# Eight floats of padding ahead of the large on-chip tile of a hybrid decoder kernel

## The chip, the cores and the metric

The kernel runs on one core of a Trainium2 chip. Its time is the device time of one execution in microseconds (us); the median of three runs before the change is 3118.18 us (3116.29 to 3118.25). One further execution was profiled; the trace and all durations below are from it.

## The reference

The computation is a decoder trunk in float32: 256 tokens of width 1024 pass four layers, and each layer is a token mixer followed by an expert network. The mixers are, in order, HGRN2 (a gated linear recurrence in chunks), FoX (attention with a forget gate), Mamba-2 SSD, and HGRN2 again.

```
for i in range(DEPTH):                                   # 4 layers
    hn = rmsnorm(h, norm_mix[i])
    h = h + mixer_i(hn)                                  # HGRN2, FoX, SSD, HGRN2
    h = h + peer_ffn(rmsnorm(h, norm_ffn[i]), ...)
return rmsnorm(h, norm_final)

def peer_ffn(h, w_q, sub_keys, u_tab, v_tab):            # in blocks of 128 tokens
    q = (xb @ w_q).reshape(M, 8, 2, 128)                 # 8 heads, two half queries
    s = einsum('mhcd,hckd->mhck', q, sub_keys)           # 128 keys per half
    ...                                                  # top 16 of the 16 x 16 sums: idx, gates
    u = take(u_tab, idx); v = take(v_tab, idx)           # 16 experts per token and head
    act = gelu(einsum('md,mhkd->mhk', xb, u)) * gates
    return einsum('mhk,mhkd->md', act, v)
```

The expert network is what moves the bytes: for each of 256 tokens, 8 heads, 16 experts and 4 layers one row of u (1024 floats) and one of v is read from a table in HBM, 8 KB together, and each row is used once.

## The kernel before

**Storage.** Nearly everything that lives in the on-chip memory lies in one tile of 196,864 bytes per partition, called `arena` (line 208), cut by hand into pieces (lines 206 to 212): the residual stream `h`, two transposed or repeated copies of the tokens (`xT`, `XR`), the keys, the scores `SS`, a work area `mix` for the mixers, `kept` (eight places of 8 KB that hold weights across the two token blocks of a layer) and `gb` (seven buffers of 8 KB). The tile is the fourth of its pool, behind the constants `cst` (3,136 bytes per partition), the parameters `par` (1,544) and the identity with the norm weights `fst` (768). Two streaming buffers `raw` of 8 KB per partition lie in a pool behind it, and the small working tiles in another behind that. Each piece of `arena` has a length that is a multiple of 256 bytes, so all pieces begin at the same place within a block of 256 bytes as the tile itself. In the program as built, `arena` begins at byte 7,648 of each partition, which is 29 blocks of 256 bytes and 224 bytes more; the `raw` buffers begin at bytes 205,024 and 213,216, also 224 bytes past a multiple of 256. Places are given out in steps of 32 bytes.

**Gathers.** A pair is 2 × 64 tokens with two experts each. For each half of a pair (`g`), `fetch` (line 1519) takes a free buffer of 8 KB per partition from a deque `ring`, and GpSimd issues one indirect DMA (line 1517) that brings 128 rows of 8 KB, u and v side by side, one row into each partition: 1 MB. The buffers of the ring are the seven of `gb`, and those of the eight kept places that no weight holds at the time. The last pair of all is fetched in six smaller gathers (`fetch_last`).

**What is done with a buffer.** `dot` (line 1550): VectorE multiplies the u half with the token's row and sums it (the call at line 1554, recorded at the helper's line 229). `active`: ScalarE applies the gelu and scales a 128 × 64 matrix with it (line 242). `spread` (line 1574): TensorE multiplies that matrix with the v half into the accumulators (line 1587), after which the buffer goes back to the ring (line 1590). The loop over pairs (line 1713) has 64 pairs in each of 8 stages; a stage is one block of 128 tokens of one layer.

**Beside it.** While one stage gathers, the mixer and the queries of the next run in pieces between the pairs (`side`, `products_`, `others`), by a table of costs. Their weights come in units of 1 MB through SyncE's queue (line 413), into the two `raw` buffers, the kept places, or, in the beginning, other pieces of the arena. The routing of the next heads (top 16, indices, gates) runs in steps on VectorE (`route_steps`). The order of all instructions on each engine is fixed when the program is built.

Of the kernel before, what the change touches and what calls it, by code (L numbers as in the profile page):

```python
# [11 lines left out]
F32 = mybir.dt.float32  # L12
# [7 lines left out]
P = 128  # L20
# [169 lines left out]
def trunk(ctx: ExitStack, tc: tile.TileContext, d: dict, out: bass.AP):  # L190
    nc = tc.nc
    SB = bass.MemoryType.PSUM
    cpool = ctx.enter_context(tc.tile_pool(name="c", bufs=1))
# [11 lines left out]
    fst = cpool.tile([P, P + 8 * 2 * DEPTH], F32, name="fst")  # L205
    sizes = (("h", D), ("xT", D), ("XR", 2 * D), ("keys", UNIT), ("SS", 2048), ("mix", MIX), ("kept", NKEPT * UNIT),
             ("gb", NGB * 2 * D))
    arena = cpool.tile([P, sum(n for _, n in sizes)], F32, name="arena")
    at_, o_ = {}, 0
    for name, n in sizes:  # L210
# [1556 lines left out]
```

## Time and profile before

| what | number |
|---|---|
| median of three runs | 3118.18 us |
| the profiled execution | 3123.27 us, its span from the first to the last instruction 3121.4 us |
| instructions | 34,341 |
| mean granted TensorE clock | 0.942 |
| busy: TensorE, VectorE, ScalarE, GpSimd | 83%, 67%, 50%, 39% of the span |
| moved by DMA | 1266.60 MB, mean 406 GB/s |
| gathers | 1028 indirect DMAs, 1073.81 MB |
| loads and stores through SyncE's queue | 190.60 MB |

The page of the profile gives busy times of the engines, the span in 40 equal slices (a digit is a share in tenths, GB/s is what the DMA moved in that slice), the DMA queues with their packets, the chain of work that ended last, and the groups of instructions. A packet is one piece of a transfer that one of the core's 16 DMA engines carries out: here a row of a partition, or the four bytes that report a DMA's end. Since every DMA over 128 partitions is spread over 16 engines, each of them gets 8 rows and one such report. The share of a queue is the sum of its packets' times over 16 engines times the stretch; records of neighbouring packets overlap a little, so it can pass 100%.

### The profile page before, as it was taken

How to read it: one execution, taken by the hardware profiler on the slowest of the kernel's cores; microseconds unless marked ns; L12 is line 12 of the kernel's file. 1: busy time of each engine (PE TensorE's matmuls, PEld its weight loads, DVE VectorE, ACT ScalarE, POOL GpSimd, SP SyncE). 2: the span in 40 equal slices, each digit the busy share in tenths (PEclk: the TensorE clock that was granted, in tenths of full speed). 3: DMA queues.
4: the chain of work that ended last, by engine and by line, in shares of the span. 5: the costliest groups of instructions: out<-in, count | busy, mean ns of one | idle time of the engine just before them, and what ended most of it. 6: DMA issues, size and time to landing. Idle time of an engine off the chain costs nothing.

```text
span 3121.4 us, 34341 instructions
## 1 busy us (share of the span) xinstructions
PE 2592.7 (83%) x10170; PEld 1106.6 (35%) x10170; DVE 2103.5 (67%) x5583; ACT 1563.6 (50%) x4485; POOL 1202.7 (39%) x1036
## 2 busy tenths in 40 slices
PE   9899877987789996898878998869887899876666
PEld 4444342332234552344324543523222343521111
DVE  1677657765857766888486885577657677677754
ACT  3465434463445643688245784346444655443433
POOL 0244334443433342433243333334334333455454
PEclk9999988999899998999989999989989999999999
DMA  8799999999999999999999999999999999999998
GB/s 339 280 418 420 419 419 414 414 407 420 411 412 419 386 416 419 391 418 420 388 419 411 407 419 383 412 413 401 419 420 419 410 408 419 419 419 420 420 420 345
DMA packets 176184, 1266.60 MB, mean 406 GB/s; under 512 B 19584, under 2 KB 20224, under 8 KB 22912
## 3 DMA queue, kind: packets, MB, share of 16 engines
q0 software_dynamic: 147776, 1073.81, 83.8%
q1 hardware_dynamic: 28224, 190.60, 14.9%
q8 instruction: 84, 1.38, 0.2%
q14 instruction: 100, 0.82, 0.1%
HBM read 1263.28 MB, written 1.05 MB: 405 GB/s over the span
## 4 chain that ended last, share of the span: by engine, by line
DMA 47%; PE 18%; issue 14%; DVE 11%; POOL 5%; ACT 4%; POOLq 0%; DVEq 0%
DMA arena<-in_uv,ix 46%; PE pj L271 8%; DVE arena L229 7%; PE acc L1587 6%; POOL arena L1517 5%; PE ps L271 4%; ACT L242 2%; DMA raw<-in_ssm 1%; DVE eq L229 1%; ACT dg L242 1%; ACT arena L242 1%; PE ps L275 1%; DVE af L229 0%; DMA arena<-in_wq 0%; DVE gs L229 0%
## 5 line engine op out<-in xcount | busy, mean ns | idle before, releaser
L1517 POOL DMA_INDIRECT arena<-in_uv,ix x1028 | 1200.4, 1168 | 1902.3 <-PE acc L1587 1189.2
L229 DVE SCALAR_TENSOR_TENSOR arena<-arena 128x1024 f32<-128x1024 f32 (+2 forms) x1088 | 1267.6, 1172 | 825.4 <-DMA arena<-in_uv,ix 817.0
L1587 PE MATMUL acc<-arena,dg 128*64 128x512 f32 x4096 | 1389.0, 662 | 471.5 <-ACT dg L242 469.3
L242 ACT ACTIVATE dots<-dots 128x1 f32<-128x1 f32 x1024 | 203.0, 198 | 1242.8 <-DVE arena L229 1241.4
L1587 PEld LDWEIGHTS acc<-arena,dg 128*64 128x64 f32 x4096 | 343.2, 144 | 1333.8 <-ACT dg L242 936.1
L271 PE MATMUL pj<-arena 128*128 128x128 f32 (+1 forms) x1760 | 435.7, 400 | 1.5 <-ACT arena L242 0.8
L242 ACT ACT_TABLE_LOAD x330 | 423.4, 1283 | 6.9 <-PEq L1758 0.7
L271 PE MATMUL pj<-raw,arena 128*128 128x512 f32 x736 | 352.3, 620 | 29.6 <-DMA raw<-in_ssm 24.5
L242 ACT ACTIVATE dg<-dg,dots 128x64 f32<-128x64 f32 x1024 | 356.2, 348 | 33.2
L271 PEld LDWEIGHTS pj<-arena 128*128 128x128 f32 x1760 | 246.1, 191 | 184.4 <-issue 169.3
L242 ACT ACTIVATE dg<-m,gs 128x64 f32<-128x64 f32 x1024 | 293.8, 334 | 0.0
L271 PE MATMUL ps<-arena 128*128 128x128 f32 (+4 forms) x1696 | 232.7, 284 | 4.2 <-DMA arena<-in_wq 2.1
L271 PEld LDWEIGHTS ps<-arena 128*128 128x128 f32 (+3 forms) x1696 | 188.6, 177 | 107.5 <-issue 54.6
L271 PEld LDWEIGHTS pj<-raw,arena 128*128 128x128 f32 x736 | 134.6, 194 | 244.9 <-issue 209.2
L242 ACT ACTIVATE arena<-ps 128x256 f32<-128x256 f32 (+4 forms) x186 | 64.8, 391 | 45.3 <-PE ps L271 44.7
L229 DVE DVE_READ_ACCUMULATOR arena<-arena 128x1 f32 x1024 | 83.8, 82 | 0.0
L271 PE MATMUL ps<-cst,arena 128*128 128x128 f32 (+2 forms) x320 | 73.3, 343 | 0.4 <-DVE arena L229 0.4
L275 PEld LDWEIGHTS ps<-fst,arena 128*128 128x128 f32 x440 | 51.5, 146 | 58.4 <-issue 36.4
L275 PE MATMUL ps<-fst,arena 128*128 128x128 f32 x440 | 70.5, 288 | 0.7 <-DVE arena L229 0.7
L229 DVE FIND_INDEX8 si<-sv,arena 128x8 uint32<-128x128 f32 x256 | 69.8, 284 | 0.0
L229 DVE MAX8 sv<-arena 128x8 f32<-128x128 f32 x256 | 61.5, 282 | 4.0 <-ACT arena L242 4.0
L229 DVE SCALAR_TENSOR_TENSOR arena<-arena,cst 128x128 f32<-128x128 f32 x224 | 62.3, 345 | 0.3
(132 smaller groups left out, 1415.3 us busy)
## 6 DMA issues: line engine op xcount, KB each, us to landing
raw<-in_ssm SPq DMA_DIRECT2D x48, 1024.0 KB, 9.3
arena<-in_hg SPq DMA_DIRECT2D x31, 1024.0 KB, 19.7
raw<-in_hg SPq DMA_DIRECT2D x30, 1024.0 KB, 9.3
arena<-in_wq SPq DMA_DIRECT2D x21, 1024.0 KB, 10.0
arena<-in_uv,ix POOLq DMA_INDIRECT x1028, 13.3
raw<-in_fox SPq DMA_DIRECT2D x14, 1024.0 KB, 9.6
raw<-in_wq SPq DMA_DIRECT2D x9, 1024.0 KB, 9.1
arena<-in_fox SPq DMA_DIRECT2D x9, 1024.0 KB, 14.8
```

Of the source, the lines that this page charges most:

```text
L229: return getattr(nc.vector, name)(o, *a, **k)
L242: nc.scalar.activation(o, i, f, **k)
L271: nc.tensor.matmul(o, w, m, start=start, stop=stop)
L275: nc.tensor.transpose(o, i, ident)
L1517: nc.gpsimd.indirect_dma_start(o, None, src, bass.IndirectOffsetOnAxis(ap=ix, axis=0))
L1587: nc.tensor.matmul(accs[s][e][g * 64:g * 64 + 64], dg[:, g], v, start=False, stop=hh == 7 and q == NQ - 1)
```

## The change

One tile of eight floats (32 bytes) per partition, which nothing reads or writes, is put between `fst` and `arena`. In the program as built `arena` then begins at byte 7,680 (30 × 256), the `raw` buffers at 205,056 and 213,248 (801 and 833 × 256); with them every piece of `arena`, the seven ring buffers and the kept places begin at multiples of 256 bytes. The small tiles behind move up by 32 bytes too; `cst`, `par` and `fst` stay. The sequence of instructions on each of the five engines is the same, row for row, with shapes and order unchanged; only line numbers behind line 207 grow by one.

```
     sizes = (("h", D), ("xT", D), ("XR", 2 * D), ("keys", UNIT), ("SS", 2048), ("mix", MIX), ("kept", NKEPT * UNIT),
              ("gb", NGB * 2 * D))
+    cpool.tile([P, 8], F32, name="pad")
     arena = cpool.tile([P, sum(n for _, n in sizes)], F32, name="arena")
     at_, o_ = {}, 0
     for name, n in sizes:
```

More of the change, by code (lines that the diff above doesn't have):

```diff
@@ L207, in trunk @@
              ("gb", NGB * 2 * D))
+    cpool.tile([P, 8], F32, name="pad")
     arena = cpool.tile([P, sum(n for _, n in sizes)], F32, name="arena")
```

## The prediction

> **What bounds the kernel now.** I read first the page's slices, queues and DMA total.
>
> ```profile
> PE 2592.7 (83%) x10170; PEld 1106.6 (35%) x10170; DVE 2103.5 (67%) x5583; ACT 1563.6 (50%) x4485; POOL 1202.7 (39%) x1036
> ...
> GB/s 339 280 418 420 419 419 414 414 407 420 411 412 419 386 416 419 391 418 420 388 419 411 407 419 383 412 413 401 419 420 419 410 408 419 419 419 420 420 420 345
> DMA packets 176184, 1266.60 MB, mean 406 GB/s; under 512 B 19584, under 2 KB 20224, under 8 KB 22912
> ...
> q0 software_dynamic: 147776, 1073.81, 83.8%
> q1 hardware_dynamic: 28224, 190.60, 14.9%
> ```
>
> Most slices stand at 418 to 420 GB/s and none passes that; in between are dips to 383 or 391. At 420 GB/s the 1266.60 MB would take 1266.60 / 0.420 = 3016 us of the span's 3121.4: all but 105 us is at the pace of the transfers. No engine is as full as that. Then the chain of work that ended last:
>
> ```profile
> DMA 47%; PE 18%; issue 14%; DVE 11%; POOL 5%; ACT 4%; POOLq 0%; DVEq 0%
> DMA arena<-in_uv,ix 46%; PE pj L271 8%; DVE arena L229 7%; PE acc L1587 6%; POOL arena L1517 5%; PE ps L271 4%; ACT L242 2%; DMA raw<-in_ssm 1%; DVE eq L229 1%; ACT dg L242 1%; ACT arena L242 1%; PE ps L275 1%; DVE af L229 0%; DMA arena<-in_wq 0%; DVE gs L229 0%
> ```
>
> By this only 47% of the span, 1467 us, is surely transfer time; the rest goes through engines, beside transfers that are nearly always busy. So what a cheaper transfer is worth lies between 47% and 97% (3016 of 3121) of what it saves in transfer time. The groups say how much room the engines leave:
>
> ```profile
> L1517 POOL DMA_INDIRECT arena<-in_uv,ix x1028 | 1200.4, 1168 | 1902.3 <-PE acc L1587 1189.2
> L229 DVE SCALAR_TENSOR_TENSOR arena<-arena 128x1024 f32<-128x1024 f32 (+2 forms) x1088 | 1267.6, 1172 | 825.4 <-DMA arena<-in_uv,ix 817.0
> L1587 PE MATMUL acc<-arena,dg 128*64 128x512 f32 x4096 | 1389.0, 662 | 471.5 <-ACT dg L242 469.3
> ```
>
> A pair is two gathers, 2.10 MB, 5.0 us at 420 GB/s. Its own work is 2 × 1.17 = 2.3 us on VectorE and, over the 512 pairs, 1389.0 / 512 = 2.7 us on TensorE. VectorE's idle time is ended by the gather (817.0 of 825.4 us): it waits for data. GpSimd's idle time is ended by TensorE's giving buffers back (1189.2 us), but a gather (2.5 us of transfer) lands a median of 13.3 us after it was issued, behind others in the queue, so this wait is not the bound:
>
> ```profile
> arena<-in_uv,ix POOLq DMA_INDIRECT x1028, 13.3
> ```
> In the last stage almost nothing but gathers is left, and I take from there what a row costs.
>
> ```profile
> 0.00:400.00 400.00, 362.47 (x1466) 173.43 (x1467) 236.16 (x658) 189.85 (x499) 120.85 (x110) 0.97 0.92 376
> 400.00:800.00 400.00, 321.83 (x1252) 131.27 (x1250) 265.71 (x717) 187.88 (x580) 160.62 (x138) 0.91 1.01 414
> ...
> 1200.00:1600.00 400.00, 335.49 (x1240) 137.94 (x1240) 301.92 (x830) 236.65 (x633) 144.65 (x128) 0.94 1.00 407
> ...
> 2830.00:3000.00 170.00, 108.21 (x270) 25.82 (x270) 117.81 (x304) 67.93 (x228) 84.21 (x68) 0.92 1.01 420
> ```
>
> (The columns are the stretch, busy us of TensorE, its weight loads, VectorE, ScalarE and GpSimd, the granted clock, the DMA share and GB/s.) In the middle TensorE is busy 322 to 362 of 400 us and transfers run at 407 to 414 GB/s, so there a gain is partly lost to engines. I set the share that comes through at 0.7, between 0.47 and 0.97.
>
> **The change part by part.** No instruction is added, removed or moved in order; no wait is added; nothing is issued for the padding. What changes is where rows begin: 224 bytes past a multiple of 256 before, at a multiple now. That touches (a) each row written by gathers and loads, (b) rows read by the output stores, (c) where engines read and write. The number of rows: 1266.60 MB / 8192 bytes / 16 = 9663 rows of 8 KB per DMA engine, counting smaller ones by their bytes. So a nanosecond per row is 9.7 us of transfer time, and 4.5 to 9.4 us of the kernel's, 6.8 at a share of 0.7.
>
> No transfer of before writes an on-chip row at a multiple of 256 bytes. I bound (a) by the nearest rows. First what a packet costs beside its bytes, from two stretches: rows of 8 KB at 224 (gathers alone), and rows of 1 KB into the parameter tile, which in the built program begin at byte 5,312, 192 past a multiple of 256.
>
> ```profile
> DMA packets 9798, 71.36 MB, mean 420 GB/s; under 512 B 1089, under 2 KB 1089, under 8 KB 1089
> ...
> q0 software_dynamic: 9791, 71.29, 101.2%
> ```
>
> ```profile
> DMA packets 241, 1.23 MB, mean 425 GB/s; under 512 B 32, under 2 KB 99, under 8 KB 99
> ...
> q0 software_dynamic: 158, 1.16, 97.0%
> q1 hardware_dynamic: 83, 0.07, 7.1%
> ```
>
> The first is 2830 to 3000 us: 101.2% of 16 × 170 us is 2752.6 us for 71.29 MB in 9791 packets. The second is 1211.5 to 1214.4 us: queue 1 has 83 packets; 99 − 32 = 67 of them are rows of 1 KB (68,608 bytes), 16 are reports of four bytes; 7.1% of 16 × 2.9 us is 3.294 us. With a time per byte a and a time per packet c, 71.29e6 a + 9791 c = 2752.6 us and 68,608 a + 83 c = 3.294 us give c = 8.8 ns and a = 0.0374 ns, so 306.4 + 8.8 = 315 ns for a row of 8 KB. Now two stretches against this line: rows of 4 KB written at 224 (715.5 to 727.1 us, queue 1), and the first half's stores (3052 to 3058.3 us, queue 1), whose rows of 2 KB are written to HBM at multiples of 2 KB.
>
> ```profile
> q0 software_dynamic: 526, 3.80, 79.1%
> q1 hardware_dynamic: 272, 1.05, 22.3%
> ```
>
> ```profile
> q0 software_dynamic: 293, 2.13, 80.1%
> q1 hardware_dynamic: 284, 0.52, 21.6%
> ```
>
> The 256 rows of 4 KB: 39.2 + 272 × 0.0088 = 41.6 us by the line, 22.3% of 16 × 11.6 = 41.4 us measured, 0.9 ns less per row. The 256 rows of stores: 19.6 + 2.5 = 22.1 us by the line, 21.6% of 16 × 6.3 = 21.8 us measured, 1.3 ns less per row. A row whose written end lies on multiples of 256 is thus 0.4 ns cheaper than the line has it for rows at 224, with about that much in the rounding of the shares. This is the nearest row to the change, so I take **0 for the price of where a row begins, with 0.4 ns (2 to 4 us) as its own uncertainty**. It is not proof: the stores read their on-chip end at 224, which could hide a gain.
>
> The bound below is that the whole time per packet goes for rows, 8.8 ns: 9663 × 8.8 = 85 us of transfer time. The bound above comes from the last fence: beside the stores, 260 gathered rows and 33 reports took 80.1% of 16 × 6.3 = 80.7 us where the line gives 79.7 + 2.6 = 82.2, so each row was 5.8 ns quicker than among loads alone. Transfers into the chip slow each other by that much, and the new places could change it either way by as much: 56 us of transfer time.
>
> [...]
>
> (b) is 32 packets on each engine in all, four stores of 128 rows: 32 × 8.8 ns is 0.3 us at most, and only the last two stores end the kernel. (c): engines read and write the same shapes 32 bytes further on; no row differs by where it lies in a way that I can see, and the engines' idle shares (17% for TensorE, 33% for VectorE) cover small changes; 0. If a vector product of 1172 ns did lose or gain 1%, 12 ns on each of some 1028 is 12 us of VectorE time, hidden in its 825 us of waiting for gathers.
>
> The sum is 0: the profiled execution would stay at its 3123.27 us (span 3121.4 and 1.9 around it), 5.1 above the median of the runs shown, and the forecast for the median is 3118, with 3112 to 3123 as this case's own range.
>
> **The rivals.**
>
> *Rows lose their whole packet time* (faster, much). For it: a packet costs 8.8 ns, and the same part of a block of 256 bytes is open at both ends of each row now; a row at 224 touches 33 blocks, one at 0 only 32, which by itself is 1/33 = 3.0%, about the 8.8 of 315 ns. Against: rows at 192 and 224 and stores that end on boundaries cost the same per packet; reports of four bytes must cost it too for the sums above to hold. Price 85 us × 0.7 = 59 (40 to 82): 3059. [...]
>
> *The crowding of loads eases* (faster, a little). The 5.8 ns among loads would be partly the 33rd block of each row that the chip's side has to take. For it: it goes where half of the packets are stores. Against: those stores also take reads off HBM, where the new places change nothing. Half of it, 2.9 ns, is 28 us of transfer time, 20 of the kernel's: 3098; all of it, 39: 3079.
>
> *The crowding gets worse* (slower). [...] It decides from 0.9 ns per row (6.2 us). For it: only that the price exists. Against: before, all buffers lay at 224 alike, so nothing moved against anything else; the distance between `arena` and `raw` is unchanged.
>
> That the change does not do what it says is excluded by the built program's places.
>
> **How the numbers follow.** A measurement of this kernel can tell 0.2% (6.2 us) from nothing. No price: 0.66 (0.62 within 0.2%, 0.02 on either side). Whole packet time: 0.10. Crowding eases: 0.16 (0.02 of it within 0.2%). Crowding worse: 0.08. So faster 0.02 + 0.10 + 0.14 = 0.26, same 0.64, slower 0.10. The range 3082 to 3128 holds the first case, nearly all of the easing and the mildest of the worsening, about 0.83; it leaves out the first rival and most of the third.
>
> **What would show it.** If right, the stretch of gathers alone near the end still stands at 420 GB/s, gathers there land as late as before, queue 0's share per packet stays at 2752.6 us per 9791 packets, and the slices peak at 420. If rows lose their packet time, that stretch and the full slices rise to about 420 × 315 / 306 = 432 GB/s, and the dips in the middle become more, with VectorE's wait for gathers well under 817 us. If crowding eases, the stretch rises by 1 to 2% and its per-row time nears the 309 ns seen beside the stores (315.2 − 5.8); if it worsens, it falls below 416. A changed mean of the vector products (1172 ns) or matrix products (662 ns) at an equal clock would show that I was wrong on (c). The forecast is wrong if the median leaves 3112 to 3124.

## The result: 1.5% faster, and the profile after

The changed kernel takes 3070.86 us (median of 4 runs, 3069.05 to 3074.24) against 3117.74 us before. The ratio is 0.9852 with a 95% interval of 0.9835 to 0.9869: 47 us less. The forecast was no change, at 3118. The profiled execution of the changed kernel took 3071.52 us, its span 3069.7.

The page of the changed kernel: busy times, the 40 slices, the DMA total.

```profile
PE 2580.6 (84%) x10170; PEld 1102.6 (36%) x10170; DVE 2100.2 (68%) x5583; ACT 1562.5 (51%) x4485; POOL 1224.0 (40%) x1036
...
GB/s 344 268 421 421 427 426 426 421 420 427 423 417 426 393 420 426 394 426 427 403 426 414 406 423 408 420 422 395 427 427 426 419 425 427 421 427 427 427 426 357
DMA packets 176184, 1266.60 MB, mean 413 GB/s; under 512 B 19584, under 2 KB 20224, under 8 KB 22912
```

The same bytes in the same packets, but full slices stand at 426 to 427 GB/s where they stood at 418 to 420. The stretch of gathers alone, 2830 to 3000 us, shows it without anything else:

```profile
DMA packets 9954, 72.53 MB, mean 427 GB/s; under 512 B 1104, under 2 KB 1104, under 8 KB 1104
...
q0 software_dynamic: 9946, 72.44, 100.9%
```

Before, this stretch moved 71.29 MB of gathers in 9791 packets at 101.2%. Now 72.44 MB / 8192 = 8843 rows took 100.9% of 16 × 170 us, 2744.5 us; less 8.8 ns for each of 1103 reports of four bytes that is 309.3 ns per row of 8 KB, against 315.2 before. These are times from the packets' records, which overlap a little. By the pace (the engines' time divided by the rows carried, so that an overlap is not counted twice) a row takes 16 × 170 / 8843 = 307.6 ns against 312.6: **5.0 ns less per row**.

The chain of work that ended last, and the groups that the prediction named:

```profile
DMA 46%; PE 18%; DVE 14%; issue 12%; ACT 5%; POOL 4%; POOLq 0%; SPq 0%; DVEq 0%; ACTq 0%
...
L1518 POOL DMA_INDIRECT arena<-in_uv,ix x1028 | 1221.6, 1188 | 1829.7 <-PE acc L1588 1097.7
L230 DVE SCALAR_TENSOR_TENSOR arena<-arena 128x1024 f32<-128x1024 f32 (+2 forms) x1088 | 1266.2, 1172 | 775.7 <-DMA arena<-in_uv,ix 767.5
L1588 PE MATMUL acc<-arena,dg 128*64 128x512 f32 x4096 | 1374.9, 656 | 438.2 <-ACT dg L243 436.5
```

A vector product takes 1172 ns as before, a matrix product 656 instead of 662. Engines do nothing faster that matters; VectorE waits 767.5 us for gathers instead of 817.0, 49.5 less, which is the size of the whole gain.

In the middle of the kernel the gain comes through as well (columns as in the prediction's table):

```profile
400.00:800.00 400.00, 322.89 (x1254) 132.15 (x1251) 273.12 (x747) 190.75 (x593) 171.30 (x141) 0.91 1.01 424
...
1200.00:1600.00 400.00, 342.44 (x1263) 138.67 (x1261) 310.03 (x851) 243.37 (x652) 162.43 (x134) 0.95 1.00 416
```

424 and 416 GB/s where it was 414 and 407, though TensorE and VectorE have as much to do there.

It is not the gathers alone, nor GpSimd's queue. At 20 to 40 us, but for one packet of instructions, only loads from SyncE's queue run. Before:

```profile
DMA packets 1150, 8.38 MB, mean 419 GB/s; under 512 B 128, under 2 KB 128, under 8 KB 128
```

And in the changed kernel:

```profile
DMA packets 1170, 8.54 MB, mean 427 GB/s; under 512 B 128, under 2 KB 128, under 8 KB 128
```

### The profile page after: what moved, and what is told of

Its sections match the earlier page's. It is cut to its first block, busy times and chain, and to the rows that moved or that the text cites. A ratio compares the mean times of both kernels' runs of the same rounds, so it can differ in the third digit from the quotient of the medians.

```text
span 3069.7 us, 34341 instructions
## 1 busy us (share of the span) xinstructions
PE 2580.6 (84%) x10170; PEld 1102.6 (36%) x10170; DVE 2100.2 (68%) x5583; ACT 1562.5 (51%) x4485; POOL 1224.0 (40%) x1036
## 2 busy tenths in 40 slices
DMA packets 176184, 1266.60 MB, mean 413 GB/s; under 512 B 19584, under 2 KB 20224, under 8 KB 22912
## 4 chain that ended last, share of the span: by engine, by line
DMA 46%; PE 18%; DVE 14%; issue 12%; ACT 5%; POOL 4%; POOLq 0%; SPq 0%; DVEq 0%; ACTq 0%
DMA arena<-in_uv,ix 45%; DVE arena L230 10%; PE pj L272 7%; PE acc L1588 6%; PE ps L272 5%; POOL arena L1518 4%; ACT L243 2%; DVE eq L230 1%; ACT dg L243 1%; ACT arena L243 1%; PE ps L276 1%; DMA raw<-in_ssm 1%; DVE af L230 1%; DVE si L230 0%; DVE gs L230 0%
## 5 line engine op out<-in xcount | busy, mean ns | idle before, releaser
L1518 POOL DMA_INDIRECT arena<-in_uv,ix x1028 | 1221.6, 1188 | 1829.7 <-PE acc L1588 1097.7
L230 DVE SCALAR_TENSOR_TENSOR arena<-arena 128x1024 f32<-128x1024 f32 (+2 forms) x1088 | 1266.2, 1172 | 775.7 <-DMA arena<-in_uv,ix 767.5
L1588 PE MATMUL acc<-arena,dg 128*64 128x512 f32 x4096 | 1374.9, 656 | 438.2 <-ACT dg L243 436.5
```

The source lines that it names most:

```text
L230: return getattr(nc.vector, name)(o, *a, **k)
L1518: nc.gpsimd.indirect_dma_start(o, None, src, bass.IndirectOffsetOnAxis(ap=ix, axis=0))
L1588: nc.tensor.matmul(accs[s][e][g * 64:g * 64 + 64], dg[:, g], v, start=False, stop=hh == 7 and q == NQ - 1)
```

## The experiments

After the result I held four theories of the price. **W**: a row that does not begin at a multiple of 256 bytes on the chip touches one block of 256 more (33 instead of 32), and this costs about 5 ns whatever the offset. **H**: a smaller boundary, 64 or 128 bytes, is enough. **O**: the price grows with the distance from the multiple of 256 below up to the start, so that a start at 32 pays a seventh of what one at 224 pays (47 / 7 = 7 us, an estimate). And a rival of another kind, **S**: the gain belongs to the small tiles or to what engines read, which moved too. All ratios are against the kernel before, on the same chip, with the 95% interval behind.

### Which of the moved things it is

```
-    cpool.tile([P, 8], F32, name="pad")
     arena = cpool.tile([P, sum(n for _, n in sizes)], F32, name="arena")
+    cpool.tile([P, 8], F32, name="pad")
```

> The pad of 8 floats stands behind the large tile: the streaming buffers and all small tiles lie where the changed kernel has them, but the arena with ring and kept places stays at 224. If the gain belongs to the large rows written (W, H or O alike), only the 101 transfers of 1 MB into the streaming buffers gain, 8.4% of the bytes: 4 us, about 3114. If it came from the small tiles or from what engines read: about 3071.

Measured: 0.9988 (0.9978 to 0.9998), 3.3 us less by the medians. The small tiles lie here where the changed kernel has them, and nearly all of the gain is missing, so it does not belong to them. What is there has the size that 8.4% of the bytes would give, but it lies at the edge of the noise.

The time alone does not clear the other half of S, since what engines read in the arena did not move here either. The trace does. From 1215 to 1480 us all loads of SyncE's queue go into the streaming buffers, which moved, while the gathers beside them go to places that did not. The loads before, and in this run:

```profile
q1 hardware_dynamic: 2448, 17.83, 16.2%
```

```profile
q1 hardware_dynamic: 2579, 18.88, 16.9%
```

Before, 2177 rows of 8 KB and 271 reports took 16.2% of 16 × 265 us, 314.4 ns a row; here 2305 rows and 274 reports took 309.8 ns a row, each figure with about 1 ns in the rounding of the share. Counted packet by packet in the two traces, 17% of these rows took 309 ns before and 71% here; of the gathered rows in the same stretch it was 19% and 28%. Rows that moved became quicker among rows that did not, beside engines that read the arena where they did before. S falls: it is the rows that transfers write.

### Which boundary

The pad before the arena is made 16, 24, 40 or 56 floats instead of 8, so that all large rows begin 32, 64, 128 or 192 bytes past a multiple of 256.

```
-    cpool.tile([P, 8], F32, name="pad")
+    cpool.tile([P, 16], F32, name="pad")        # 24, 40, 56
```

> A pad of 16 floats instead of 8: all large rows begin 32 bytes past a multiple of 256. If any start off a multiple of 256 costs a 33rd block (theory W), the gain is gone: about 3118 us and 420 GB/s in the stretch of gathers alone. If only multiples of 64 matter (theory H): 3118 as well. [...] If the gain came from something else in the small tiles, no clear forecast.

> A pad of 24 floats: rows begin 64 bytes past a multiple of 256. Theory W (33rd block): about 3118 us, 420 GB/s. Theory H (multiples of 64 suffice): about 3071, 427 GB/s. [...]

> A pad of 40 floats: rows begin 128 bytes past a multiple of 256. Theory W: about 3118 us, 420 GB/s. Theory H, or a rule of 128 bytes: about 3071, 427 GB/s. [...]

> A pad of 56 floats: rows begin 192 bytes past a multiple of 256. Offsets of 32, 64, 128 and 224 gave 0.1% more, 0.2% less, 0.3% less and 0 against the kernel before. If the price depends on how short the shorter end piece of a row is, 192 (a first piece of 64 bytes) is as 64: about 3108 us. If it is the same for any start off the boundary, 3115 to 3118.

Measured:

| start past a multiple of 256 | ratio to before | interval |
|---|---|---|
| 0 (the change) | 0.9852 | 0.9835 to 0.9869 |
| 32 | 1.0008 | 0.9998 to 1.0018 |
| 64 | 0.9978 | 0.9969 to 0.9988 |
| 128 | 0.9972 | 0.9961 to 0.9984 |
| 192 | 0.9973 | 0.9963 to 0.9983 |
| 224 (before) | 1 | |

The stretch from 2830 to 3000 us, for 32:

```profile
DMA packets 9795, 71.36 MB, mean 420 GB/s; under 512 B 1087, under 2 KB 1087, under 8 KB 1087
```

for 64:

```profile
DMA packets 9834, 71.62 MB, mean 421 GB/s; under 512 B 1094, under 2 KB 1094, under 8 KB 1094
```

for 128:

```profile
DMA packets 9832, 71.64 MB, mean 421 GB/s; under 512 B 1089, under 2 KB 1089, under 8 KB 1089
```

and for 192:

```profile
DMA packets 9837, 71.63 MB, mean 421 GB/s; under 512 B 1096, under 2 KB 1096, under 8 KB 1096
```

All four are near 420, none near 427. H falls, and so does O: a start at 32 bytes cost as much as one at 224 (1.0008 against 1), and one at 128 cost less (0.9972). What is left is the boundary of 256 bytes that W names, with a second, small effect: at 64, 128 and 192, where the shorter piece at an end of a row is 64 or 128 bytes, 7 to 10 us came back; at 32 and 224, where it is 32 bytes, nothing did. The case of 192 was foreseen from 64 by the length of the shorter end piece, 3108, and measured 3107.30. Whether the 33rd block is the reason stays open: every start off the boundary adds a block and makes both end pieces short, and no run has one without the other.

### Off a multiple of 32

The pad of the change stays, and the arena begins 16 bytes into its tile: its rows begin 16 bytes past a multiple of 256, those of the streaming buffers 32 bytes past.

```
     cpool.tile([P, 8], F32, name="pad")
-    arena = cpool.tile([P, sum(n for _, n in sizes)], F32, name="arena")
+    arena = cpool.tile([P, 8 + sum(n for _, n in sizes)], F32, name="arena")[:, 4:]
```

> [...] If only the 33rd block counts (W): about 3118 us, as at 32 bytes. [...]

Measured: 3127.23 us, 1.0028 (1.0015 to 1.0041). This is about 9 us on top of the kernel before. The stretch from 2830 to 3000 us:

```profile
DMA packets 9757, 71.09 MB, mean 418 GB/s; under 512 B 1082, under 2 KB 1082, under 8 KB 1082
...
q0 software_dynamic: 9750, 71.01, 101.1%
```

71.01 MB are 8668 rows, by the pace 313.8 ns each, 1.2 more than the 312.6 before. Against the start at 32 bytes (1.0008, 0.9998 to 1.0018) it is some 6 us, and the intervals just touch. It may be a price of a start within 32 bytes, or the effect of the short end piece going on, which is 16 bytes here; this run does not part the two.

### Which end of the transfer

The expert table is laid out 56 floats further on in HBM, so each gathered row begins 224 bytes past a multiple of 256 of its former place at its source.

```
-    a["uv"] = np.concatenate([peer_u.reshape(-1, D), peer_v.reshape(-1, D)], axis=1)
+    uv = np.concatenate([peer_u.reshape(-1, D), peer_v.reshape(-1, D)], axis=1)
+    z = np.zeros(2 * D, np.float32)
+    a["uv"] = np.concatenate([z[:56], uv.reshape(-1), z[56:]]).reshape(-1, 2 * D)
...
-        nc.gpsimd.indirect_dma_start(o, None, src, bass.IndirectOffsetOnAxis(ap=ix, axis=0))
+        nc.gpsimd.indirect_dma_start(o, None, src, bass.IndirectOffsetOnAxis(ap=ix, axis=0), element_offset=56)
```

> The pad as in the change, so all on-chip rows begin at multiples of 256; but the expert table in HBM is laid out 56 floats further on, so that each gathered row begins 224 bytes past a multiple of 256 at its source. Theory D (only the written end counts): about 3071 us, 427 GB/s among gathers alone. Theory R (the two ends must begin at the same place within 256 bytes): about 3112, 420 GB/s, since gathers are 85% of the bytes. Theory E (each end off the boundary costs by itself): 3112 or more.

> No pad, and the table laid out 56 floats further on: gathered rows begin 224 bytes past a multiple of 256 at both ends. Theory D: as the kernel before, about 3117 us, 420 GB/s among gathers alone. Theory R: about 3077, 427 GB/s there (weights still go from 0 to 224). Theory E: slower than before by as much again, up to 3157, 413 GB/s there.

Measured: with the pad 0.9848 (0.9828 to 0.9867), without it 1.0000 (0.9990 to 1.0010). Gathers alone with the pad and the moved table:

```profile
DMA packets 9968, 72.58 MB, mean 427 GB/s; under 512 B 1112, under 2 KB 1112, under 8 KB 1112
```

and without the pad:

```profile
DMA packets 9793, 71.34 MB, mean 420 GB/s; under 512 B 1087, under 2 KB 1087, under 8 KB 1087
```

For these gathers only the written end on the chip counts; that the table's former place is itself at a multiple of 256 is assumed here. Neither the read end nor whether both ends agree made a difference that 0.2% can show: with the table moved the ratio is 0.9848 beside the change's 0.9852, and 1.0000 without the pad.

### A larger boundary

```
-    cpool.tile([P, 8], F32, name="pad")
+    cpool.tile([P, 72], F32, name="pad")
```

> A pad of 72 floats: the ring buffers and kept places begin at multiples of 8 KB, the streaming buffers at multiples of 256. If the boundary of 256 bytes is the whole of it: as the changed kernel, about 3071 us. If a larger boundary counts too (4 or 8 KB, which a row now crosses once or not at all): up to another 47 us less, 3024.

> The changed kernel as it is, on the same chip as the others: about 3071 us, ratio to the kernel before 0.985.

Measured: 0.9852 (0.9833 to 0.9871) with the ring and the kept places at multiples of 8 KB, 0.9855 (0.9836 to 0.9875) for the change itself. A larger boundary gains nothing that 0.2% can show. No variant beats the change.

### Per row or per byte

```
-        gather(home[n], d["uv"], got[s, hh][0][:, g, q:q + 1])
+        for k, nm in enumerate("uv"):
+            gather(home[n][:, k * D:(k + 1) * D], d[nm], got[s, hh][0][:, g, q:q + 1])
```

> No pad; the expert table is laid out as two, u and v, and each gather is made as two with rows of 4 KB (the split of the last pair is left out). 8224 more rows and 1028 more reports per DMA engine at 8.8 ns are about 81 us more. If the price of a start at 224 is one 33rd block per row (theory W), it doubles for the gathers: 3118 + 81 + 8224 x 5.5 ns = 3244 us, 92 above split_0. If it goes by bytes (each block of 256 bytes costs a little more): 3199, 47 above split_0.

> The same split with the pad of the change: 3071 + 81 = 3152 us by either theory, if transfers still set the pace and GpSimd's 2056 gathers at 1.17 us (2405 us) don't. The gap to split_224 decides: 92 us per row, 47 per byte.

Measured: 3237.92 us at 224 and 3215.22 at 0, a gap of 23 us, less than either theory. The times do not answer the question, because the condition in the expectation failed: transfers no longer set the pace. The groups on GpSimd in the kernel with the pad:

```profile
L1518 POOL DMA_INDIRECT arena<-in_u,ix x1024 | 1132.2, 1106 | 520.7 <-issue 218.5 <-DVE ix L230 109.2 <-DMA arena<-in_u,ix 92.8
L1518 POOL DMA_INDIRECT arena<-in_v,ix x1024 | 1117.4, 1091 | 424.6 <-issue 236.0 <-DMA arena<-in_v,ix 69.6 <-PE acc L1586 55.9
```

Of their 945 us of idle time 455 are "issue", in which the engine waited for nothing that the profile shows; in the kernel before, 1189.2 of 1902.3 us were waits for buffers. GpSimd is busy with gathers for 2250 of 3215 us here, and the stretch from 2830 to 3000 us runs at 371 GB/s (at 224) and 380 (at 0), well under full. But there are stretches in which gathers of 4 KB rows do fill the DMA engines. At 224, 3170 to 3210 us:

```profile
q0 software_dynamic: 4499, 16.37, 102.6%
```

At 0, 3150 to 3190 us:

```profile
q0 software_dynamic: 4611, 16.79, 102.6%
```

16.37 MB are 3997 rows of 4 KB in 40 us on 16 engines, 160.1 ns each; 16.79 MB are 4099 rows, 156.1 ns each. A row of half the length pays 4.0 ns, where the long one pays 5.0 and a price by bytes would be 2.5. It is not the choice of the two stretches: over all stretches of 20 us in which such rows keep the DMA engines over 101.5% busy (26 at 224 and 24 at 0), the medians are 160.8 and 156.8 ns. So the price lies between the two theories, nearer to one per row; it is not a fixed price of a row, as W had it.

## Why the prediction was wrong

**What was right.** The bound: DMA sets nearly all of the time, 3016 of the span's 3121.4 us at 420 GB/s. Nothing was added, moved or waited for; the vector and matrix products kept their durations (c); the output stores did not matter (b): 84 ns a row of 2 KB before and after. The rival "the crowding of loads eases" is what happened, and not by half, which the forecast took for its middle, but in full: it was priced at 5.8 ns per row at most, and the gathers' rows fell by 5.9 ns in the records and 5.0 in the pace. The mark it was given, a rise of the stretch by 1 to 2%, is the 427 for 420. The cause that it supposed, the 33rd block of each row, is neither shown nor excluded by the runs.

**The step that failed** is the value taken for (a), with 0.4 ns as its uncertainty: "This is the nearest row to the change, so I take 0". The runs put it at 5.9 ns per row of 8 KB in the records, 5.0 in the pace. The stores were the only rows written at multiples of 256, and the line they were held against was drawn through rows that all bear the price. With the rows after, it can be seen. Two stretches of the changed kernel, from 1193.6 to 1196.8 us (1 KB rows into the parameter tile) and 2698.2 to 2701.7 us (128 rows of 4 KB):

```profile
DMA packets 269, 1.37 MB, mean 427 GB/s; under 512 B 35, under 2 KB 112, under 8 KB 112
...
q1 hardware_dynamic: 94, 0.08, 7.2%
```

```profile
q1 hardware_dynamic: 128, 0.52, 36.3%
```

The second is 20.33 us for 128 rows, 158.8 ns each. The same load before, 2742.4 to 2746 us:

```profile
q1 hardware_dynamic: 130, 0.52, 36.0%
```

which is 20.74 us, 161.9 ns each after two reports. In the first, 77 rows of 1 KB and 17 reports took 7.2% of 16 × 3.2 us, 3.69 us: 45.9 ns a row where the prediction's stretch had 47.1. So 1 KB fell by about 1, 4 KB by 3, 8 KB by 6, while the stores stay at 84 ns: now 286 packets took 22.3% of 16 × 6.1 us, 21.77 us from 3001.5 to 3007.6 us, the same as before.

```profile
q0 software_dynamic: 285, 2.07, 80.4%
q1 hardware_dynamic: 286, 0.52, 22.3%
```

The stores lay 1.3 ns below the line and the 4 KB rows 0.9 below, and I took the difference of 0.4 as the price. But the 4 KB rows carried 3 ns of it themselves. A line drawn through loaded rows cannot show what they have in common, and here a short row said little about a long one. The evidence that did answer stood in the same fence: 8 KB rows beside the stores were 5.8 ns quicker. I read it as a bound of contention in general and not as a level that rows can have everywhere. In the first row of the last fence, the same place after the change, 253 rows take (80.4% of 16 × 6.1 us less 32 reports) 309.0 ns beside the stores, against 309.3 among loads alone: the difference of 5.8 ns is gone.

**Against the first rival**, the packet time of 8.8 ns did not go. The time of a row fell to 309 ns, and the short rows and the reports still show a time per packet: 46 ns for 1 KB and 309 for 8 KB leave 8.4 ns beside the bytes, and 19,577 of the 19,585 reports take 9 ns in the changed kernel, as 18,550 did before; the mark for that rival, 432 GB/s, was not reached. The 33rd block was named there, with 3.0% as its price; the runs show 5.0 of 312.6 ns, 1.6%.

**The share that comes through** was set at 0.7, between 0.47 from the chain and 0.97 from the bytes. The transfers need 1266.60 MB / 0.420 − 1266.60 / 0.427 = 49 us less, and the kernel takes 47 us less: 0.95. The share was set low in part by the engines' load in the middle, and of the "322 to 362" us given for it the 362 is the first stretch, at 376 GB/s; the two rows shown from the middle have 322 and 335. With the DMA engines full at nearly all times (busy for 90% or more in 37 of the 40 slices before), the bytes at the peak pace were the better measure than the chain's share. With the full 5.8 ns and that share the rival would have come to 3118 − 56 × 0.95 = 3065.

**The range** began at 3082, because the easing was taken at about half of its bound and, in full, left out. The measured 3071 lies between this rival in full (3079) and the first rival (3059). The worsening that its upper end, 3128, made room for is shown by no run: with the change the rows became 5.0 ns quicker.

## What the runs showed of the hardware that was not expected

Rows that did not move gained too. The 1 KB rows above go into the parameter tile, which did not move and begins 192 bytes past the boundary in both kernels; they became 1 ns cheaper (47.1 to 45.9 ns) when the rows beside them were moved to the boundary. Counted over the whole traces, 92 of the 128 rows of 1 KB took 46 ns before, and all 128 after. In the run with the pad behind the arena, the gathers that did not move gained a little beside loads that did (19% to 28% at 309 ns), and the loads, though on the boundary, were at 309 ns only to 71%, where the changed kernel has 98% in the same stretch.

Nor is the price a fixed addition to each row. Of the rows gathered to 224 bytes, 18% took 309 ns in the kernel before, as 98% do after the change; 46% took 313 and 13% took 320. In stretches of 10 us in which the DMA engines were busy for less than 97%, 58% of the 8 KB rows took 309 ns in the kernel before; where they were busy for 100% or more, 13% did. And beside the stores, with the engines full (80.1% and 21.6% by the two queues), 234 of 260 gathered rows took 309 ns before, and all 253 do now. So in these traces a start off the boundary cost most where the engines were full of rows like it, and the 5 ns are a mean. Why that is so, no run here shows. That gathered rows read off the boundary cost nothing that shows (0.9848 beside 0.9852), and that 32 bytes cost as much as 224 (1.0008), was not expected either.

## What to carry to other kernels

Where a kernel runs at the peak pace of its transfers, look at where the rows begin that they write on the chip: 32 bytes of padding, which cost no instruction, gave 1.5% here, and a pool that packs tiles in steps of 32 bytes leaves it to chance. Before a price of zero is taken from a comparison of rows, ask whether each of them bears the price already; here the gathered rows beside the stores took 309.4 ns before, what rows came to after (309.3). And where the DMA engines are full nearly throughout, take a cheaper transfer at its bytes, not at its share of the chain: here 0.95 of it came through, where the chain had 0.47.
